# Five pairs of merge gate blocks as seven products of half matrices, computed ahead of the keys, values and queries

## The chip, the cores and the metric

The kernel runs on one core of a Trainium2 chip. The metric is the device time of one execution in microseconds (us). The core's engines run side by side, each through its own list of instructions in a fixed order: PE multiplies matrices (and loads the stationary operand, PEld), DVE (VectorE) and ACT (ScalarE) work elementwise, POOL (GpSimd) as well, and SP mainly issues DMA transfers. An instruction starts when the one before it on its engine is through and what it waits for on other engines and transfers has happened.

## The reference

One decoder layer for 1024 tokens of width 1024. A normalised input `h` is multiplied by `w_in`; the 3768 columns of the product feed two token mixers in parallel (NSA with compressed, selected and window attention; MLA with low-rank queries and keys) and the merge gates, which are the last 2048 columns. The gates weigh the two mixers, then come an output projection and a gated feed-forward part.

```
h = _rmsnorm(x, g_pre_mix[i])
proj = h @ w_in[i]
q_n, kv_n, gate_n, c_q, c_kv, k_r, merge = jnp.split(proj, offsets, axis=-1)
...
gm = jax.nn.sigmoid(merge...).reshape(B, T, 2, D)
merged = gm[:, :, 0] * (o_nsa @ w_br_nsa[i]) + gm[:, :, 1] * (o_mla @ w_br_mla[i])
x = x + _rmsnorm(merged @ w_o[i], g_post_mix[i])
h = _rmsnorm(x, g_pre_ffn[i])
u = _causal_dwconv(h @ w_up[i], w_conv[i], b_conv[i])
a, v = u[..., :D_FF], u[..., D_FF:]
x = x + _rmsnorm((jax.nn.gelu(a) * v) @ w_down[i], g_post_ffn[i])
```

## The kernel before

Precision: every float32 factor is held as two halves, a high one (`hh`, `whi`, `rh`, ...) and a low one (`hl`, `wlo`, `rl`, ...), and a product is three matmuls, high by high, high by low and low by high (`mm3`, L191). The halves come from `split_evac` (L197): ACT copies the value to the high half, then DVE subtracts the high half from the value. So each split is an ACT and a DVE instruction, in that order, and the second waits for the first. `h` lies transposed, features on partitions, as `hh[c]`, `hl[c]` for the two halves `c` of the tokens; the program prints them as `hh_122`, `hh_124` (high) and `hl_123`, `hl_125` (low).

Weights: `Weights` (L53) is a queue. A raw block of 128 columns (1024 rows, 512 KB) is loaded by SP into one of three buffers `wraw`, split into `whi`/`wlo` (two buffers each), and its raw buffer is given back (`done`). The queue runs in the order in which items are added.

A projection of one block, `fproj` (L436 to L449), is 2 token halves x 8 row blocks x 3 = 48 matmuls of 128x512. For a merge gate, `merge_evac` (L451) lets ACT take the sigmoid out of PSUM and issues the store to `gm_d`. There are sixteen such gate blocks.

The order of the work before: the input is normalised, gate 0 is computed, then MLA's queries, keys and values (`mla_q`, `mla_qt`, `mla_v`, `mla_k`, L488 to L543), which store their results to DRAM from SP (`q_d` L517, `v_d` L526, `k_d` L535, from the tiles `qx`, `vm`, `kx`, two buffers each). Gates 1 and 2 follow (L557), then the compressed keys (`kcT`), keys, values and queries, then gates 3 to 13 (L672), then attention, in which gates 14 and 15 are computed. When MLA's pool is closed behind it, its memory is given to later tiles; such a tile can be written once the store that reads the old one has landed.

Seven products: the up projection of the feed-forward part already multiplies pairs of blocks in this way (L1158 to L1450). A pair is the 1024 x 256 matrix of two column blocks, `a` and `v`; with the 1024 tokens it is a product of a 2 x 2 by a 2 x 2 matrix of halves. Instead of eight half products it uses seven, P1 to P7: the weights give sums S1 to S4 (`block_sum`), the tokens give sums T1 to T4 (`t_blocks`, L1239 to L1267, once), each sum is split into high and low, and the seven results are added up (U2, U3, C). One half product is 12 matmuls of 128x512, so a pair is 84 matmuls instead of 96. `prep` splits the next product's weight halves into `rh`, `rl` (4 buffers), 4 products ahead.

The order on each engine is set when the program is built: a scheduler that knows the operations' costs reorders the written order, within buffers and data dependences.

Of the kernel before, what the change touches and what calls it, by code (L numbers as in the profile page):

```python
# [17 lines left out]
T = 1024  # L18
# [111 lines left out]
        return self.items[i].hl  # L130


def attend(units, fills):
# [27 lines left out]
    for _, _, f in sorted(ev, key=lambda e: e[:2]):  # L161
        f()
# [3 lines left out]
def tile_hybrid_layer(ctx: ExitStack, tc: tile.TileContext, x, p, positions, g_pre_mix, w_in,  # L166
# [87 lines left out]
    for c0 in [0, 128, 256, 384] + [1720 + 128 * m for m in range(NM, 16)]:  # L254
# [193 lines left out]
    def fproj(evac):  # L448
        fproj2([evac])  # L449
# [219 lines left out]

    for f in range(4):  # L670
        fproj(q_evac(f))
    for m in range(NM, 14):  # L672
        fproj(merge_evac(m))


    def slope(h):
# [475 lines left out]
    def flat(ps):  # L1152
# [1 line left out]

    lo_k, hi_k = slice(0, 4), slice(4, 8)  # L1158
    block = dict(P1="A11", P2="A12", P3="S4", P4="A22", P5="S1", P6="S2", P7="S3")
    SEQ = [(f, p, block[p]) for f in range(1, NF)  # L1160
           for p in (("P1", "P6", "P7", "P5", "P2", "P4", "P3") if f > 1 else ("P1", "P2", "P3", "P5", "P6", "P7", "P4"))]
    WT, SS = {}, {}
    RING = 4

    def halves(src):
        hl = [ring([128, 4, 128], F32R, tag, bufs=RING) for tag in ("rh", "rl")]
        split_evac(*hl, src)
        return hl

    def pair(f):  # L1170
        return [it.raw.rearrange("p (k m) -> p k m", m=128) for it in up_pairs[f]]

    def block_sum(f, i):

        a, v = pair(f)
        out_ = SS[f, i] = ring([128, 4, 128], F32, f"S{i}")
        first, second, op = ((v[:, lo_k], v[:, hi_k], OP.add), (SS.get((f, 0)), a[:, lo_k], OP.subtract),
                             (a[:, lo_k], v[:, lo_k], OP.subtract), (a[:, hi_k], SS.get((f, 1)), OP.subtract))[i]
        nc.vector.tensor_tensor(out_, first, second, op=op)

    def prep(n):

        if n >= len(SEQ):
            return
        f, _, name = SEQ[n]
        a, v = pair(f)
        WT[n] = halves(SS[f, int(name[1]) - 1] if name[0] == "S" else
                       a[:, lo_k] if name == "A11" else a[:, hi_k] if name == "A12" else v[:, hi_k])
        if name in ("A12", "A22"):
            W.done()  # L1190
# [41 lines left out]
    takes = dict(P1="B11", P2="B21", P3="B22", P4="T4", P5="T1", P6="T2", P7="T3")  # L1232
# [6 lines left out]
    def t_blocks():  # L1239
# [29 lines left out]
    def product(ps, n, more=False):  # L1269
        wh, wl = WT.pop(n)  # L1270
        bh, bl = BB[takes[SEQ[n][1]]]
        for k in range(4):
            mm3(ps, wh[:, k], wl[:, k], bh[:, k], bl[:, k], not more and k == 0, k == 3, more)
# [101 lines left out]

    low, high = slice(2, 514), slice(514, 1026)
    for i in range(4):
        block_sum(1, i)
    X = [big(), big()]
    for c in (1, 0):  # L1380
        for s in range(2):
            for h, name in enumerate((("B11", "B21"), ("B12", "B22"))[c]):
                (wh, wl), (bh, bl) = W0[s][h], BB[name]
                for k in range(4):
                    mm3(X[s][:, c], wh[:, k], wl[:, k], bh[:, k], bl[:, k], h == k == 0, h == 1 and k == 3)
                if c == 0:
                    prep(2 * s + h)
    for s in range(2):
        nc.scalar.activation(CC[0][s][:, 2:], flat(X[s]), AF.Copy)
    t_blocks()  # L1390
    pieces = conv_pieces(0, CC[0])
    for f in range(1, NF):
        C = CC[f % 2]
        X = big()
        for s in range(7):
            n = 7 * (f - 1) + s
            pr = SEQ[n][1]
            if pr == "P1":
                product(X[:, 0], n)
            elif pr == "P2":  # L1400
                product(X[:, 0], n, more=True)
            elif pr == "P5":
                product(X[:, 1], n)
            elif pr == "P3" and f > 1:
                product(X[:, 1], n, more=True)
            elif pr == "P3":
                first = one()
                product(first, n)
            elif pr == "P6":
                six = one()  # L1410
                product(six, n)
            elif pr == "P7":
                seven = one()
                product(seven, n)
            else:
                product(seven, n, more=True)
            prep(n + RING)
            if s < 4 and f + 1 < NF:
                block_sum(f + 1, s)
            for run in pieces[s]:  # L1420
                run()
            if pr == "P1":
                e1 = ep([128, 512], F32, "e1")
                nc.scalar.activation(e1, X[:, 0], AF.Copy)  # L1424
            elif pr == "P2":
                nc.scalar.activation(C[0][:, low], X[:, 0], AF.Copy)
            elif pr == "P3" and f > 1:
                nc.vector.tensor_tensor(C[0][:, high], X[:, 1], U2, op=OP.add)
            elif pr == "P3":
                e3 = ep([128, 512], F32, "U3")  # L1430
                nc.scalar.activation(e3, first, AF.Copy)
            elif pr == "P6":
                U2 = ep([128, 512], F32, "U2")
                nc.vector.tensor_tensor(U2, six, e1, op=OP.add)
                if f == 1:
                    nc.vector.tensor_tensor(C[0][:, high], X[:, 1], U2, op=OP.add)
                    nc.vector.tensor_tensor(C[0][:, high], C[0][:, high], e3, op=OP.add)
            elif pr == "P7":
                U3 = ep([128, 512], F32, "U3")
                nc.vector.tensor_tensor(U3, seven, U2, op=OP.add)  # L1440
            if pr == ("P5" if f > 1 else "P7"):
                nc.vector.tensor_tensor(C[1][:, high], X[:, 1], U3, op=OP.add)
            elif pr == "P4":
                nc.vector.tensor_tensor(C[1][:, low], seven, U2, op=OP.add)
# [227 lines left out]
```

## Time and profile before

| what | us |
|---|---|
| median of three runs | 1791.93 (1789.28, 1799.06, 1791.93) |
| the profiled execution | 1793.26 |
| its span | 1791.5 |
| PE busy | 1724.0 (96%), 8585 matmuls |
| DVE busy | 1196.9 (67%) |
| ACT busy | 837.7 (47%) |
| POOL busy | 308.5 (17%) |

Busy times overlap. The span is the time from the first to the last instruction of the profiled execution; 1.8 us of the execution's time lies around it. The mean granted TensorE clock was 0.989 of full speed. In the profile a row names line, engine, operation and tiles (output, then inputs); "[2.10 <-DVE vm L199]" behind a row means that the engine had been idle for 2.10 us, and that the wait ended with the DVE instruction of line 199 that wrote `vm`.

### The profile page before, as it was taken

What the parts mean: (1) busy time and instruction counts of PE and PEld (TensorE: products, weight loads), DVE (VectorE), ACT (ScalarE), POOL (GpSimd) and SP (SyncE); (2) the same over time, 40 slices, a digit from 0 to 9 for tenths busy, and PEclk for the clock granted to TensorE, in tenths of its full rate; (3) what the DMA queues carried; (4) which work ended last, traced back from release to release, by engine and by line L of the source; (5) the groups of instructions that cost most, each with busy time, mean ns of one, the idle gap of its engine ahead of it and who ended that gap; (6) DMA issues with size and microseconds to landing.
All of it is one profiled execution on the core that took longest, in us unless ns stands there. A gap on an engine that the chain in (4) does not pass through costs nothing.

```text
span 1791.5 us, 23480 instructions
## 1 busy us (share of the span) xinstructions
PE 1724.0 (96%) x8585; PEld 1411.1 (79%) x8585; DVE 1196.9 (67%) x1875; ACT 837.7 (47%) x1498; POOL 308.5 (17%) x467
## 2 busy tenths in 40 slices
PE   8979999999999999999999989999999998999998
PEld 6868978887787787887778867888888876887886
DVE  6543431116888888787764787888888879768553
ACT  6442322115777766666542434444444443335321
POOL 3132000003555553333311000000000000001010
PEclk9999999999999999999999999999999999999999
DMA  5385122320001316657372112222223292438111
GB/s 193 89 245 143 48 58 84 94 77 24 2 1 36 106 58 181 151 146 190 110 252 99 36 59 87 79 82 94 72 83 95 71 340 94 137 117 291 55 59 47
DMA packets 182511, 191.94 MB, mean 107 GB/s; under 512 B 12804, under 2 KB 136124, under 8 KB 182396
## 3 DMA queue, kind: packets, MB, share of 16 engines
q1 hardware_dynamic: 175292, 180.91, 33.1%
q10 hardware_dynamic: 7104, 9.54, 1.7%
q8 instruction: 68, 1.11, 0.3%
q14 instruction: 47, 0.39, 0.1%
HBM read 142.96 MB, written 47.45 MB: 106 GB/s over the span
## 4 chain that ended last, share of the span: by engine, by line
PE 77%; DVE 8%; DMA 7%; ACT 3%; issue 2%; POOL 1%; SPq 1%; ACTq 0%; DVEq 0%; POOLq 0%
PE big L194 9%; PE big L193 9%; PE big L195 9%; PE pT L193 7%; PE pT L195 7%; PE pT L194 7%; PE pT L734 5%; PE one L193 3%; PE one L194 3%; PE one L195 3%; PE oT L744 3%; PE oT L743 3%; PE sc L797 1%; DVE wlo L199 1%; PE sc L790 1%
## 5 line engine op out<-in xcount | busy, mean ns | idle before, releaser
L235 POOL TENSOR_SCALAR stat<-stat 128x1 f32<-128x1 f32 (+1 forms) x48 | 19.4, 404 | 898.3 <-ACT yn L1130 632.2
L199 DVE TENSOR_TENSOR pl<-pT,ph 128x512 fp32r<-128x512 f32 (+1 forms) x244 | 149.4, 629 | 13.7 <-ACT ph L198 12.0
L198 ACT ACTIVATE ph<-pT 128x512 fp32r<-128x512 f32 (+1 forms) x244 | 130.1, 555 | 60.7 <-PE pT L734 52.9
L193 PE MATMUL pT<-hh,whi 128*128 128x512 f32 x384 | 151.4, 394 | 5.2 <-DVE vm L199 2.1
L195 PE MATMUL pT<-hh,wlo 128*128 128x512 f32 x384 | 151.0, 393 | 0.0
L194 PE MATMUL pT<-hl,whi 128*128 128x512 f32 x384 | 151.0, 393 | 0.0
L193 PE MATMUL big<-hh,rh 128*128 128x512 f32 x364 | 142.1, 391 | 2.0 <-ACT e L1424 0.8
L195 PE MATMUL big<-hh,rl 128*128 128x512 f32 x364 | 141.6, 390 | 1.0 <-DVE rl L199 1.0
L194 PE MATMUL big<-hl,rh 128*128 128x512 f32 x364 | 141.8, 390 | 0.0
L718 DVE TENSOR_REDUCE mx<-sc 128x1 f32<-128x640 f32 (+7 forms) x128 | 106.5, 834 | 34.6 <-PE sc L797 24.7
L107 DVE TENSOR_TENSOR wlo<-wraw,whi 128x1024 fp32r<-128x1024 f32 x26 | 31.9, 1226 | 140.8 <-ACT whi L106 140.7
L1286 DVE SCALAR_TENSOR_TENSOR u<-C,wcT,u 128x1024 f32<-128x1024 f32 x88 | 110.8, 1278 | 3.4 <-ACT u L1282 3.4
L194 PE MATMUL big<-wlo,whi 128*128 128x512 f32 x242 | 97.5, 403 | 9.4 <-DVE wlo L199 9.3
L198 ACT ACTIVATE rh<-S 128x512 fp32r<-128x512 f32 x84 | 52.6, 629 | 99.9 <-PE big L194 85.3
L195 PE MATMUL big<-whi,wlo 128*128 128x512 f32 x242 | 96.1, 397 | 0.0
L193 PE MATMUL big<-whi 128*128 128x512 f32 x242 | 92.2, 397 | 1.2 <-ACT whi L198 1.2
L193 PEld LDWEIGHTS pT<-hh,whi 128*128 128x128 f32 x384 | 72.9, 190 | 21.5 <-DVE vm L199 2.5
L198 ACT ACTIVATE rh<-wraw 128x512 fp32r<-128x512 f32 x67 | 41.9, 630 | 92.7 <-PE big L194 41.8
L195 PEld LDWEIGHTS pT<-hh,wlo 128*128 128x128 f32 x384 | 72.9, 190 | 15.3
L194 PEld LDWEIGHTS pT<-hl,whi 128*128 128x128 f32 x384 | 72.8, 190 | 15.1
L193 PEld LDWEIGHTS big<-hh,rh 128*128 128x128 f32 x364 | 68.2, 188 | 17.7 <-ACT e L1424 1.2
L195 PEld LDWEIGHTS big<-hh,rl 128*128 128x128 f32 x364 | 68.3, 188 | 15.6 <-DVE rl L199 1.4
(484 smaller groups left out, 4769.1 us busy)
## 6 DMA issues: line engine op xcount, KB each, us to landing
wraw<-in_w_up_dram SPq DMA_DIRECT2D x44, 512.0 KB, 3.8
wraw<-in_w_in_dram SPq DMA_DIRECT2D x24, 512.0 KB, 4.3
g<-gm_d SPq DMA_DIRECT2D x48, 256.0 KB, 3.2
wraw<-in_w_down_dram SPq DMA_DIRECT2D x47, 256.0 KB, 3.2
g_d<-u SPq DMA_DIRECT2D x22, 512.0 KB, 2.8
wraw<-g_d SPq DMA_DIRECT2D x36, 256.0 KB, 3.3
xt<-in_x_dram SPq DMA_DIRECT2D x16, 512.0 KB, 6.9
gm_d<-gms ACTq DMA_DIRECT2D x16, 512.0 KB, 3.0
```

The costliest lines, as they stand in the source:

```text
L107: nc.vector.tensor_sub(lo, raw, f32(hi))
L193: nc.tensor.matmul(ps, lh, rh, start=start, stop=False, skip_group_check=more)
L194: nc.tensor.matmul(ps, lh, rl, start=False, stop=False, skip_group_check=more)
L195: nc.tensor.matmul(ps, ll, rh, start=False, stop=stop, skip_group_check=more)
L198: nc.scalar.activation(hi, ps, AF.Copy)
L199: nc.vector.tensor_sub(lo, ps, f32(hi))
L235: nc.gpsimd.tensor_scalar(st, st, EPS, None, op0=OP.add)
L718: nc.vector.tensor_reduce(u.nm[:, r:r + 1], src, axis=AX.XY, op=OP.max, negate=True)
L734: nc.tensor.transpose(pT[:m, r], cols(r), ident)
L743: nc.tensor.matmul(oT[:, a:], v, ph, start=first, stop=False)
L744: nc.tensor.matmul(oT[:, a:], v, pl, start=False, stop=last)
L1286: nc.vector.scalar_tensor_tensor(u[s], C[s][:, 2 - sh:2 - sh + T], wcT[:, 2 - sh, ch:ch + 1], u[s], op0=OP.mult, op1=OP.add)
```

## The change

The seven products become a class `Seven`, which the feed-forward part now uses as well, with the orders `FIRST` for its first pair and `LATER` for the others as before. A second user of the class is new: gates 3 to 12, as five pairs. For them the token sums T1 to T4 are made by `t_block` on DVE (three additions or subtractions of 128x1024 for each half, then a split), through one buffer `sum`. Gates 1, 2 and 13 stay plain blocks, and all of this comes directly behind MLA; gates 14 and 15 stay in attention. The tiles lie in three pools, `tA` (T1 to T4), `ringA` (S0 to S3, `rh`, `rl`, a fourth raw buffer) and `eA` (`sum` and the parts of the result). The sigmoid of a quarter is taken out of PSUM, of the other three after the additions.

```diff
+class Seven:
+    TAKES = dict(P1=("A11", "B11"), P2=("A12", "B21"), P3=("S4", "B22"), P4=("A22", "T4"),
+                 P5=("S1", "T1"), P6=("S2", "T2"), P7=("S3", "T3"))
+    FIRST = ("P1", "P2", "P3", "P5", "P6", "P7", "P4")
+    LATER = ("P1", "P6", "P7", "P5", "P2", "P4", "P3")
+    RING = 4
...
+    def halves(self, src):
+        hl = [self.ring([128, 4, 128], F32R, tag, bufs=self.RING) for tag in ("rh", "rl")]
+        self.split(*hl, src)
+        return hl
...
+    def product(self, ps, n, more=False):
+        wh, wl = self.WT.pop(n)
+        bh, bl = self.BB[self.TAKES[self.seq[n][1]][1]]
+        for k in range(4):
+            self.mm3(ps, wh[:, k], wl[:, k], bh[:, k], bl[:, k], not more and k == 0, k == 3, more)
+
+    def pair(self, f, X, bank, ep, C, c11, hook):
...
-    NM = 3
-    for c0 in [1720 + 128 * m for m in range(1, NM)] + [512, 640, 768, 1024]:
+    EARLY, PAIRED = (1, 2, 13), range(3, 13)
+    for m in EARLY:
+        W.add(Item(in_cols(1720 + 128 * m), 1024))
+    gate_pairs = [[W.add(Item(in_cols(1720 + 128 * m), 1024, custom=True)) for m in (m_, m_ + 1)] for m_ in PAIRED[::2]]
+    for c0 in [512, 640, 768, 1024]:
         W.add(Item(in_cols(c0), 1024))
...
+    def t_block(out_, plus, minus):
+        for ks in (slice(0, 2), slice(2, 4)):
+            (ah, al), (bh, bl) = ([f32(b[:, ks]) for b in BA[n]] for n in (plus, minus))
+            sum_ = eA([128, 2, 512], F32, "sum")
+            nc.vector.tensor_tensor(sum_, ah, bh, op=OP.subtract)
+            nc.vector.tensor_tensor(sum_, sum_, al, op=OP.add)
+            nc.vector.tensor_tensor(sum_, sum_, bl, op=OP.subtract)
+            split_evac(BA[out_][0][:, ks], BA[out_][1][:, ks], sum_)
+
+    fproj(merge_evac(EARLY[0]))
+    t_block("T1", "B12", "B11")
+    fproj(merge_evac(EARLY[1]))
+    t_block("T2", "B22", "T1")
+    t_block("T3", "B22", "B12")
+    fproj(merge_evac(EARLY[2]))
+    for i in range(4):
+        gates7.block_sum(0, i)
+    for n in range(Seven.RING):
+        gates7.prep(n)
+    t_block("T4", "B21", "T2")
+    for f in range(len(gate_pairs)):
+        tl = [gmp([128, T], F32, "gms", bufs=2) for _ in range(2)]
+        gates7.pair(f, two_banks(), bank, eA, [(c[:, :512], c[:, 512:]) for c in tl],
+                    lambda out_, ps: nc.scalar.activation(out_, ps, AF.Sigmoid), lambda s: None)
+        nc.scalar.activation(tl[1], tl[1], AF.Sigmoid)
+        nc.scalar.dma_start(gm_d[PAIRED[2 * f + 1]], tl[1])
+        nc.scalar.activation(tl[0][:, 512:], tl[0][:, 512:], AF.Sigmoid)
+        nc.scalar.dma_start(gm_d[PAIRED[2 * f]], tl[0])
...
-    for m in range(1, NM):
-        fproj(merge_evac(m))
...
-    for m in range(NM, 14):
-        fproj(merge_evac(m))
```

On DVE, behind MLA's last split (`qx`), the kernel before splits a weight block and then clears the tiles of the compressed keys and the queries:

```order
L199 TENSOR_TENSOR kx<-pT,kx 128x512
L199 TENSOR_TENSOR qx<-sc,qx 96x8x128
L107 TENSOR_TENSOR wlo<-wraw,whi 128x1024
L631 MEMSET KAc_1314 128x64
L632 MEMSET KBc_1316 128x64
```

At the same place the changed kernel has the sums of the weights (`S`, L170), of the tokens (`sum`, L675 to L677) and the splits (L309):

```order
L309 TENSOR_TENSOR qx<-sc,qx 96x8x128
L107 TENSOR_TENSOR wlo<-wraw,whi 128x1024
L170 TENSOR_TENSOR S_1532<-wraw 128x512
L170 TENSOR_TENSOR S_1536<-wraw 128x512
L170 TENSOR_TENSOR S_1534<-S_1532,wraw 128x512
L309 TENSOR_TENSOR T1l<-sum,T1h 128x1024
L309 TENSOR_TENSOR rl<-wraw,rh 128x512
L170 TENSOR_TENSOR S_1538<-wraw,S_1534 128x512
L309 TENSOR_TENSOR rl<-wraw,rh 128x512
L675 TENSOR_TENSOR sum<-hh_122,hh_124 128x1024
```

From the second `S` to the last `T4l` there are 59 such instructions in a row on DVE, 30 of 128x512 and 29 of 128x1024, and none of other work but the first additions of the results.

On PE, behind the plain blocks, the kernel before goes on with `hh`, `hl` by `whi`, `wlo` (compressed keys):

```order
L195 MATMUL pT<-hh_124,wlo 128x512
L193 MATMUL pT<-hh_122,whi 128x512
L194 MATMUL pT<-hl_123,whi 128x512
L195 MATMUL pT<-hh_122,wlo 128x512
L193 MATMUL pT<-hh_122,whi 128x512
```

In the changed kernel the products of the first pair stand there; P1 and P3 take halves of `h`, and the 25th matmul takes T2:

```order
L303 MATMUL pT<-hh_122,rh 128x512
L304 MATMUL pT<-hl_123,rh 128x512
L305 MATMUL pT<-hh_122,rl 128x512
L303 MATMUL pT<-T2h,rh 128x512
L303 MATMUL sc<-hh_124,rh 128x512
L304 MATMUL sc<-hl_125,rh 128x512
```

The last product of the first pair, P4, takes T4; in front of it stand the products P1, P6, P7 and P5 of the second pair:

```order
L304 MATMUL sc<-hl_125,rh 128x512
L305 MATMUL sc<-hh_124,rl 128x512
L303 MATMUL pT<-T4h,rh 128x512
L304 MATMUL pT<-T4l,rh 128x512
L305 MATMUL pT<-T4h,rl 128x512
L303 MATMUL pT<-T4h,rh 128x512
```

From the first matmul of the first product to the first that reads the second half of T4, 126 matmuls are issued.

## Rows read from the trace of the kernel before

**Rows 1.** The page: busy time of each engine, and the chain's shares.
```profile
PE 1724.0 (96%) x8585; PEld 1411.1 (79%) x8585; DVE 1196.9 (67%) x1875; ACT 837.7 (47%) x1498; POOL 308.5 (17%) x467
...
PE 77%; DVE 8%; DMA 7%; ACT 3%; issue 2%; POOL 1%; SPq 1%; ACTq 0%; DVEq 0%; POOLq 0%
```

**Rows 2.** Stretches: us, busy per engine, PEclk, DMA share, GB/s.
```profile
core 0: us, PE busy (x) PEld busy (x) DVE busy (x) ACT busy (x) POOL busy (x), PEclk, DMA share, GB/s
...
124.85:140.00 15.15, 13.05 (x49) 10.31 (x50) 3.83 (x4) 3.86 (x6) 2.63 (x4) 0.89 0.82 220
...
229.20:404.00 174.80, 174.79 (x764) 144.42 (x765) 29.72 (x33) 39.19 (x55) 2.40 (x4) 0.99 0.27 79
...
1022.90:1062.00 39.10, 31.58 (x119) 23.32 (x117) 38.99 (x47) 18.50 (x25) 0.00 (x0) 0.92 0.17 54
1062.00:1420.00 358.00, 356.69 (x1571) 294.57 (x1571) 298.89 (x388) 162.10 (x224) 0.00 (x0) 1.00 0.26 84
```

**Rows 3.** Timeline of DVE in gates 3 to 13: start, us.
```profile
308.16 1.23 DVE L107 TENSOR_TENSOR wlo<-wraw,whi 128x1024 fp32r<-128x1024 f32 x1 [9.65 <-ACT whi L106]
...
395.20 1.23 DVE L107 TENSOR_TENSOR wlo<-wraw,whi 128x1024 fp32r<-128x1024 f32 x1 [9.65 <-ACT whi L106]
```

**Rows 4.** Timeline of ACT, one row for each pair of the feed-forward part.
```profile
1130.38 0.58 ACT L1424 ACTIVATE e<-big 128x512 f32<-128x512 f32 x1
...
1149.42 0.58 ACT L1424 ACTIVATE e<-big 128x512 f32<-128x512 f32 x1
```

**Rows 5.** Timeline of ACT, the ends of plain blocks behind MLA.
```profile
139.87 1.06 ACT L106 ACTIVATE whi<-wraw 128x1024 fp32r<-128x1024 f32 x1 [3.15 <-PE pT L194]
...
161.63 1.06 ACT L106 ACTIVATE whi<-wraw 128x1024 fp32r<-128x1024 f32 x1 [2.22 <-PE pT L194]
```

**Rows 6.** Timeline of SP: start and us of the issue of MLA's last store.
```profile
142.59 1.02 SPq L517 DMA_DIRECT2D q_d<-qx  x1
```

**Rows 7.** Line 517, the stores of qx: issue to landing.
```profile
L517 SPq DMA_DIRECT2D q_d<-qx x8: 323/1050/1767, 89.9 to 142.6; - x8
...
DMA to landing us min/median/max: 7.1/8.9/10.7
```

**Rows 8.** Timeline of DVE behind MLA.
```profile
140.96 1.23 DVE L107 TENSOR_TENSOR wlo<-wraw,whi 128x1024 fp32r<-128x1024 f32 x1 [2.99 <-ACT whi L106]
...
145.38 0.48 DVE L687 MEMSET QB<- 64x512 f32 x1 [2.19 <-DMA v_d<-vm]
```

**Rows 9.** Timeline of DVE at the start of the feed-forward pairs.
```profile
1033.41 0.69 DVE L199 TENSOR_TENSOR rl<-wraw,rh 128x512 fp32r<-128x512 f32 x1
1034.02 1.22 DVE L199 TENSOR_TENSOR T3l<-wlo,T3h 128x1024 fp32r<-128x1024 f32 x1
1035.15 1.28 DVE L1286 SCALAR_TENSOR_TENSOR u<-C,wcT,u 128x1024 f32<-128x1024 f32 x1
```

**Rows 10.** Groups of ACT in the feed-forward pairs: busy, mean ns.
```profile
L198 ACT ACTIVATE T4h<-wlo 128x1024 fp32r<-128x1024 f32 x1 | 1.1, 1058 | 1.3 <-DVE wlo L1249 1.3
```

**Rows 11.** Timeline of PE, its waits at the start of the feed-forward pairs.
```profile
1037.69 0.50 PE L195 MATMUL big<-hh,rl 128*128 128x512 f32 x1 [0.97 <-DVE rl L199]
...
1042.27 0.50 PE L193 MATMUL big<-hh,rh 128*128 128x512 f32 x1 [0.79 <-ACT e L1424]
...
1045.24 0.79 PE L195 MATMUL one<-T2h,rl 128*128 128x512 f32 x1 [2.23 <-DVE rl L199]
...
1052.34 0.47 PE L193 MATMUL one<-T4h,rh 128*128 128x512 f32 x1 [0.74 <-DVE U L1440]
...
1057.65 0.50 PE L193 MATMUL one<-T3h,rh 128*128 128x512 f32 x1 [2.33 <-DVE C L1444]
```

**Rows 12.** Stretches behind waits of PE; columns as in rows 2.
```profile
133.80:137.20 3.40, 3.40 (x10) 2.66 (x9) 0.45 (x1) 1.02 (x1) 0.00 (x0) 0.50 0.79 238
...
1045.20:1048.60 3.40, 3.36 (x8) 2.69 (x9) 3.40 (x5) 1.50 (x2) 0.00 (x0) 0.50 0.00 0
```

More of the change, by code (lines that the diff above doesn't have):

```diff
@@ L130, in get, with __init__, raw, block_sum @@
         return self.items[i].hl
+class Seven:
[4 more added lines that the diff above has]
+    RING = 4
+    def __init__(self, nc, W, pairs, ring, BB, mm3, split):
+        self.nc, self.W, self.ring, self.BB, self.mm3, self.split = nc, W, ring, BB, mm3, split
+        self.pairs, self.lo, self.hi = pairs, slice(0, 4), slice(4, 8)
+        self.seq = [(f, p) for f in range(len(pairs)) for p in (self.LATER if f else self.FIRST)]
+        self.WT, self.SS = {}, {}
+        for i, it in enumerate(it for its in pairs for it in its):
+            it.ahead = int(i > 2)
+            it.home = (ring, "wraw", 1) if i % 4 == 3 else None
+    def raw(self, f):
+        return [it.raw.rearrange("p (k m) -> p k m", m=128) for it in self.pairs[f]]
+    def halves(self, src):
+        hl = [self.ring([128, 4, 128], F32R, tag, bufs=self.RING) for tag in ("rh", "rl")]
+        self.split(*hl, src)
+        return hl
+    def block_sum(self, f, i):
+        if f >= len(self.pairs):
+            return
+        (a, v), lo, hi, SS = self.raw(f), self.lo, self.hi, self.SS
+        out_ = SS[f, i] = self.ring([128, 4, 128], F32, f"S{i}")
+        first, second, op = ((v[:, lo], v[:, hi], OP.add), (SS.get((f, 0)), a[:, lo], OP.subtract),
+                             (a[:, lo], v[:, lo], OP.subtract), (a[:, hi], SS.get((f, 1)), OP.subtract))[i]
+        self.nc.vector.tensor_tensor(out_, first, second, op=op)
+    def prep(self, n):
+        if n >= len(self.seq):
+            return
+        f, p = self.seq[n]
+        name, (a, v) = self.TAKES[p][0], self.raw(f)
+        self.WT[n] = self.halves(self.SS[f, int(name[1]) - 1] if name[0] == "S" else
+                                 a[:, self.lo] if name == "A11" else a[:, self.hi] if name == "A12" else v[:, self.hi])
+        if name in ("A12", "A22"):
+            self.W.done()
+    def product(self, ps, n, more=False):
[4 more added lines that the diff above has]
+    def pair(self, f, X, bank, ep, C, c11, hook):
+        nc, (((C11, C12), (C21, C22))) = self.nc, C
+        def add(out_, a, b):
+            nc.vector.tensor_tensor(out_, a, b, op=OP.add)
+        for s in range(7):
+            n = 7 * f + s
+            p = self.seq[n][1]
+            if p in ("P1", "P5"):
+                self.product(X[:, p == "P5"], n)
+            elif p == "P2" or p == "P3" and f:
+                self.product(X[:, p == "P3"], n, more=True)
+            elif p == "P3":
+                three = bank()
+                self.product(three, n)
+            elif p == "P6":
+                six = bank()
+                self.product(six, n)
+            elif p == "P7":
+                seven = bank()
+                self.product(seven, n)
+            else:
+                self.product(seven, n, more=True)
+            self.prep(n + self.RING)
+            if s < 4:
+                self.block_sum(f + 1, s)
+            hook(s)
+            if p == "P1":
+                e1 = ep([128, 512], F32, "e1")
+                nc.scalar.activation(e1, X[:, 0], AF.Copy)
+            elif p == "P2":
+                c11(C11, X[:, 0])
+            elif p == "P3" and f:
+                add(C12, X[:, 1], U2)
+            elif p == "P3":
+                e3 = ep([128, 512], F32, "U3")
+                nc.scalar.activation(e3, three, AF.Copy)
+            elif p == "P6":
+                U2 = ep([128, 512], F32, "U2")
+                add(U2, six, e1)
+                if not f:
+                    add(C12, X[:, 1], U2)
+                    add(C12, C12, e3)
+            elif p == "P7":
+                U3 = ep([128, 512], F32, "U3")
+                add(U3, seven, U2)
+            elif p == "P4":
+                add(C21, seven, U2)
+            if p == ("P5" if f else "P7"):
+                add(C22, X[:, 1], U3)
@@ L253, in tile_hybrid_layer @@
                        [[N_IN, 128], [128 * N_IN, 4], [256, 2], [1, 128]]), 1024))
-    for c0 in [0, 128, 256, 384] + [1720 + 128 * m for m in range(NM, 16)]:
+    for c0 in [0, 128, 256, 384] + [1720 + 128 * m for m in (14, 15)]:
         W.add(Item(in_cols(c0), 1024))
@@ L545, in tile_hybrid_layer @@
     a0.close()
+    tA = Pool("tA", side="left")
+    ringA = Pool("ringA", side="left")
+    eA = Pool("eA", side="left")
+    BA = {n: [tA([128, 4, 512], F32R, n + tag) for tag in "hl"] for n in ("T1", "T2", "T3", "T4")}
+    for c in range(2):
+        for h in range(2):
+            ks = slice(4 * h, 4 * h + 4)
+            BA[f"B{h + 1}{c + 1}"] = hh[c][:, ks], hl[c][:, ks]
+    gates7 = Seven(nc, W, gate_pairs, ringA, BA, mm3, split_evac)
+    def t_block(out_, plus, minus):
[25 more added lines that the diff above has]
+        nc.scalar.dma_start(gm_d[PAIRED[2 * f]], tl[0])
+    for pl in (eA, ringA, tA):
+        pl.close()
     vp0 = Pool("vp0", side="left")
@@ L1158, in tile_hybrid_layer @@
     lo_k, hi_k = slice(0, 4), slice(4, 8)
[L1159 to L1190, printed above, removed]
+    BB = {}
+    up7 = Seven(nc, W, up_pairs[1:], ring, BB, mm3, split_evac)
     W0 = {}
     def prep0(s):
-        raw = pair(0)[s]
-        W0[s] = halves(raw[:, lo_k]), halves(raw[:, hi_k])
+        raw = up_pairs[0][s].raw.rearrange("p (k m) -> p k m", m=128)
+        W0[s] = up7.halves(raw[:, lo_k]), up7.halves(raw[:, hi_k])
         W.done()
@@ L1267, in t_blocks @@
             put("T4", ks, total(nc.vector, ("whi", "wlo")[j], b21h, (OP.subtract, t2[j]), (OP.add, b21l)))
[L1269 to L1273, printed above, removed]
     def conv_pieces(f, C):
@@ L1377, in tile_hybrid_layer @@
     for i in range(4):
-        block_sum(1, i)
+        up7.block_sum(0, i)
     X = [big(), big()]
@@ L1393, in tile_hybrid_layer, with hook @@
         C = CC[f % 2]
[L1394 to L1419, printed above, removed]
+        def hook(s):
             for run in pieces[s]:
                 run()
[L1422 to L1444, printed above, removed]
             if f == NF - 1 and s == 2:
@@ L1449, in tile_hybrid_layer @@
                 ready(s - 4)
+        up7.pair(f - 1, big(), one, ep, [(c[:, low], c[:, high]) for c in C],
+                 lambda out_, ps: nc.scalar.activation(out_, ps, AF.Copy), hook)
         pieces = conv_pieces(f, C)
```

8 lines of the change are left out of this document (2 added, 6 removed).

## The prediction

> **What bounds the kernel now.** I read the page first. The reader is to see in it that PE is busy for 1724.0 of 1791.5 us and makes 77% of the chain, while DVE, busy for 1196.9 us, makes 8% of it [rows 1]. So a matmul taken away is worth its time wherever PE runs without a gap, and DVE costs nothing as long as PE has other work. Then I took the stretches one by one. In the one that holds gates 3 to 13, PE is busy for 174.79 of 174.80 us and DVE for 29.72: only PE counts there, and DVE has room. In the stretch right behind MLA's start of gate 1, from 124.85 to 140.00, the transfers are dense (share 0.82, 220 GB/s), and at the start of the feed-forward pairs DVE is full (38.99 of 39.10 us) and PE is not (31.58) [rows 2]. The last one is the nearest thing to the new stage that the trace has: the same seven products, with their T blocks made just in time. Last I read the pace of PE, and on SP, DVE and PE who waits for whom around the place to which the gates go.
>
> **What it removes.** In the gate stretch one block's split follows the other at equal distance: nine such rows from 308.16 to 395.20 are eight blocks, 87.04 / 8 = 10.88 us for 48 matmuls, 0.2267 us each [rows 3]. In the steady feed-forward pairs it is 1149.42 - 1130.38 = 19.04 us for 84 matmuls, 0.2267 us as well [rows 4], with PE busy for 356.69 of 358.00 us there [rows 2]. So the seven products run at the same pace once they are fed, and five pairs save 5 x 12 = 60 matmuls: 60 x 0.2267 = 13.6 us. This is the most that the change can give.
>
> **What it adds, and where.** Behind MLA, DVE gets one row of 59 instructions: the splits and sums of the first pair's weights, part of the second's, and T1 to T4. The change shows 30 of 128x512 and 29 of 128x1024. On a full DVE one starts 0.61 us behind a 128x512 (1033.41 to 1034.02) and 1.13 us behind a 128x1024 (1034.02 to 1035.15) [rows 9]; so the row takes 30 x 0.61 + 29 x 1.13 = 51.1 us. Beside it stand waits for ACT: where a T's low half follows directly on the last sum, DVE waits for ACT's copy of 1.06 us [rows 10]. That is so three times (second half of T1, first of T2, second of T4), and half so once or twice more: together about 4 us. 55 us in all.
>
> The starts of DVE in rows 9 lie closer than its durations (1.22 and 0.69 us). The Trainium skill, page VectorE: DVE Perf Modes, section The DRAIN you can't avoid, says that the next operation does not start until the pipe is empty. The trace does not agree: each of these starts comes 0.08 to 0.09 us ahead of the end of the one before. By that rule the row would be priced by durations, 30 x 0.69 + 29 x 1.22 = 56.1 us, and the end result would be 5 us later; I go by the starts.
>
> When can the row begin? Its second instruction, a weight sum, writes into memory that MLA's tiles had, and the last store to read them there is the last `q_d` of `qx`. It is issued at 142.59 [rows 6], and such a store lands 7.1 to 10.7 us after its issue, 8.9 in the median [rows 7]: 149.7 to 153.3. I take 153.3, since the transfers are dense at this time and the others of MLA are in flight beside it. That such reuse does stop DVE is seen at the same place now: a MEMSET of `QB` waits 2.19 us for `v_d<-vm` [rows 8]. What stands ahead of it, one weight split, is over at 142.2 [rows 8]. So the row is done at 153.3 + 55 = 208.4.
>
> When does PE want the results? Gate 1 ends at 139.87, and two plain blocks later, at 161.63, the third does [rows 5]; this is also the time at which the first of the seven products can start in the changed kernel, as three plain blocks stand in front. The first use of T4's second half comes 126 matmuls later: 161.6 + 126 x 0.2267 = 190.2. The weight halves for P1 and P3 (the third to the tenth instruction of the row) are ready at about 160, so PE can start, and then waits at T2, T3 and T4 in turn, since from there on it eats the blocks faster than DVE makes them. However the idle time is spread, PE stands at T4's second half at 208.4 and not at 190.2: **18.2 us** lost. On PE the whole queue is behind that wait: the other pairs, then keys, values and queries, so nothing fills it.
>
> Behind T4, DVE has some weight halves to catch up. At the same point of the feed-forward part, PE waits 0.74 us at T4 and then 2.33 us in the pair behind it [rows 11]: 3.1 us. Its bounds are 0 (the later pairs there lose nothing [rows 2]) and 7.5 us, all that PE lost in that start (39.10 - 31.58 [rows 2]).
>
> The clock: behind the 2.10 us wait at 132.69, which is one of PE's waits on MLA, and behind the 2.23 us wait at 1045.24 [rows 11], PE runs for 3.4 us at a granted clock of 0.50, that is 1.2 GHz, in place of 2.4 [rows 12]; half of it is lost, 1.7 us. Drops behind the first waits cost nothing, for PE waits again at the next T block anyway; only the one behind T4 counts: 1.7 us (bounds 0 and 1.7 for each of four waits, 6.8).
>
> **What comes at no cost.** ACT gets the copies of the sums and weights, the parts `e` and `U3` and sigmoids of SBUF; it is busy for 39.19 of 174.80 us in the gate stretch [rows 2], and only the copies in front of a DVE split are on the path (counted). SP issues as many gate weights as before, only sooner, so the next blocks come behind MLA's stores in its queue; with a share of 0.27 in the gate stretch [rows 2] there is room once MLA's stores are out. The keys, values, queries and their small loads on ACT's queue move back as a whole and keep their order; the gate stretch hid nothing that they need, since PE was full in it and DVE nearly idle. The first sums of T1 go between MLA's splits on DVE, two of them ahead of a `qx`: DVE is busy for 3.83 of 15.15 us there [rows 2], so they cost nothing, or 2 x 1.13 = 2.3 us if they meet a split for which PE waits. What the gates cover today is nothing.
>
> **Sum.** -13.6 + 18.2 + 3.1 + 1.7 = +9.4 us against the profiled execution of 1793.3 us: 1802.7. That execution lies 1.3 us above the median of the runs, 1791.9, which gives 1801.3; I say 1802.
>
> **Rivals.**
> Rival A, the cover holds (faster). If DVE could begin the row at 142 (behind the weight split) and PE's first 24 matmuls and the four products of the second pair that are drawn ahead of P4 cover most of the T blocks, PE waits about as much as at the start of the feed-forward pairs, 7.5 us, or less. For it: the scheduler placed products in front of P4 for just that; three plain blocks, 32.6 us, stand in front. Against it: the row is 55 us long, and 32.6 us of cover run mostly before it can begin. With 4 us of waits: -13.6 + 4 = -9.6, 1784.
>
> Rival B, the waits cancel the saving (no change). The store lands early (149.7), or the weight sum doesn't wait for it but only for the one before, so that DVE works through part of the row by 153: begun at 142.2, it ends at 197.2, and PE loses 7.0 at T4, with 3.1 + 1.7 behind it: -13.6 + 11.8 = -1.8; halfway between that and the forecast, +4. So 1790 to 1797, say 1794.
>
> Rival C, the clock is paid in full (slower still). Every wait of over 2 us at T2, T3 and T4 brings a stretch at half clock that is not hidden by the next wait, and one more in the pairs behind: 4 x 1.7 = 6.8 in place of 1.7, and 1807; with the bound of 7.5 for the pairs behind, 1811. For it: rows 12 stand right behind waits of 2.10 and 2.23 us. Against it: most of the time behind the first waits is waiting for DVE anyhow. The Trainium skill, page TensorE: Matmul & The Clock Gate, section HAM oscillation, describes a kernel whose matmuls come in bursts between waits and which pays for the low clock at every burst. Rows 12 agree for single waits; no run here shows a chain of them.
>
> Rival D, it doesn't do what it says: the products are not fed and PE keeps 96 matmuls a pair's time. The steady pairs of the feed-forward part [rows 4] leave this no more than a few parts in a hundred.
>
> **How the numbers follow.** The forecast (DVE's row decides, start 149.7 to 153.3 and small terms within their bounds: 1797 to 1808) gets 0.54, rival C 0.13, rival B 0.19, rival A 0.13, rival D 0.01. About 9 us, 0.5%, is what a measurement of this kernel can tell from no change (the three runs spread over 9.8 us), so the border to slower is 1801, next to the forecast; two thirds of its weight lie above: slower 0.36 + 0.13 + 0.01 = 0.50, rounded up to 0.52 for the price of rows by durations; same 0.18 + 0.19 = 0.35 less some of it, 0.34; faster 0.14. The range is 1788 to 1811: it holds the forecast, rival B and most of C, and leaves A out. The forecast's own range is 1797 to 1808.
>
> **What would show it.** In the profile after: a row of T and S instructions on DVE without gaps from about 153 to 208, its start behind a wait for `q_d<-qx`; PE's waits in front of rows with `T2h`, `T3h`, `T4l`, released by DVE, 18 us together; pairs 19.04 us apart behind them; the keys starting some 100 us later than now; no change in length behind the gates. The forecast is wrong if DVE starts on the row before 150, if PE's waits at T blocks are under 10 us together, or if PE waits at each head of the later pairs.

## The result and the profile after

The changed kernel takes 1800.52 us in the median of 20 runs, the kernel before 1789.44 us: a ratio of 1.0062, 95% interval 1.0047 to 1.0076, or 11.1 us more. The forecast was 1802 us, from +9.4. One of the 12 executions of the run with four pairs behind five plain blocks ran at a granted clock of 0.847 and took 1901.49 us; it is left out of that run's median below.

The profiled execution has a span of 1801.3 us. On the page, DVE has grown to 1274.0 us and to 10% of the chain [rows 1]:

```profile
PE 1720.6 (96%) x8525; PEld 1403.2 (78%) x8525; DVE 1274.0 (71%) x1978; ACT 860.7 (48%) x1532; POOL 310.7 (17%) x467
...
PE 75%; DVE 10%; DMA 8%; ACT 3%; issue 2%; POOL 1%; SPq 1%; DVEq 0%; POOLq 0%; ACTq 0%
```

PE has 60 matmuls fewer but is busy for only 3.4 us less, since more of them ran at half clock. Where the rest went stands in the stretches from the start of gate 1 to the fourth pair (columns as in [rows 2]):

```profile
119.46:149.00 29.54, 27.79 (x121) 22.37 (x121) 10.76 (x12) 7.98 (x11) 0.00 (x0) 1.00 0.85 235
149.00:154.58 5.58, 5.58 (x25) 4.61 (x25) 5.58 (x8) 1.64 (x3) 0.00 (x0) 1.00 0.35 91
154.58:203.62 49.04, 35.83 (x129) 26.16 (x127) 45.01 (x50) 17.01 (x24) 0.00 (x0) 0.84 0.21 65
203.62:212.20 8.58, 8.29 (x18) 5.71 (x19) 3.27 (x5) 2.14 (x3) 0.00 (x0) 0.51 0.17 63
212.20:229.00 16.80, 16.31 (x72) 13.14 (x70) 9.25 (x15) 6.63 (x11) 0.00 (x0) 1.00 0.38 118
229.00:250.00 21.00, 19.35 (x85) 15.70 (x85) 11.06 (x17) 8.04 (x12) 0.00 (x0) 1.00 0.23 70
```

The third row runs from the first matmul of the first product to the first that reads T4's second low half. The latter is one matmul further than the 126 of the section on the change, so 49.04 us stand there in place of 127 x 0.2267 = 28.8. In the fourth, PE is busy but at half clock. The last is about one pair: PE is busy for 19.35 us and has one wait.

DVE's timeline shows why. The columns are start, duration, engine, line, operation and tiles:

```profile
131.94 1.23 DVE L107 TENSOR_TENSOR wlo<-wraw,whi 128x1024 fp32r<-128x1024 f32 x1 [0.77 <-ACT whi L106]
137.51 0.69 DVE L170 TENSOR_TENSOR S<-wraw 128x512 f32<-128x512 f32 x1 [4.34 <-DMA q_d<-qx]
147.32 0.69 DVE L170 TENSOR_TENSOR S<-wraw 128x512 f32<-128x512 f32 x1 [9.12 <-DMA q_d<-qx]
147.93 0.69 DVE L170 TENSOR_TENSOR S<-S,wraw 128x512 f32<-128x512 f32 x1
...
202.34 1.22 DVE L309 TENSOR_TENSOR T4l<-sum,T4h 128x1024 fp32r<-128x1024 f32 x1 [1.12 <-ACT T4h L308]
```

The row of sums and splits waits 9.12 us for the last store of `qx`, starts at 147.32 and ends at 203.56 (202.34 + 1.22). SP issued that store at 135.99:

```profile
135.99 0.87 SPq L630 DMA_DIRECT2D q_d<-qx  x1
```

PE's waits in the same time and behind it:

```profile
149.00 0.50 PE L303 MATMUL pT<-hh,whi 128*128 128x512 f32 x1 [1.65 <-ACT gms L570]
164.56 0.80 PE L303 MATMUL pT<-T2h,rh 128*128 128x512 f32 x1 [4.38 <-ACT rh L308]
179.90 0.50 PE L303 MATMUL pT<-T3h,rh 128*128 128x512 f32 x1 [2.00 <-ACT T3h L308]
195.76 0.80 PE L303 MATMUL pT<-T4h,rh 128*128 128x512 f32 x1 [3.06 <-ACT T4h L308]
197.02 0.80 PE L304 MATMUL pT<-T4l,rh 128*128 128x512 f32 x1 [0.46 <-DVE T4l L309]
202.36 0.79 PE L303 MATMUL pT<-T4h,rh 128*128 128x512 f32 x1 [2.84 <-ACT T4h L308]
203.62 0.80 PE L304 MATMUL pT<-T4l,rh 128*128 128x512 f32 x1 [0.47 <-DVE T4l L309]
206.41 0.80 PE L303 MATMUL sc<-hh,rh 128*128 128x512 f32 x1 [0.29 <-ACT rh L308]
229.01 0.50 PE L303 MATMUL sc<-hh,rh 128*128 128x512 f32 x1 [0.49 <-ACT rh L308]
249.99 0.50 PE L303 MATMUL sc<-hh,rh 128*128 128x512 f32 x1 [1.64 <-DVE S L170]
```

All of them stand in front of a T block or a head of a pair, except the first. Most end with a copy on ACT, not with DVE; but these copies in turn wait for DVE's sums, as the last one of T4 does:

```profile
201.25 1.06 ACT L308 ACTIVATE T4h<-sum 128x1024 fp32r<-128x1024 f32 x1 [5.55 <-DVE sum L677]
```

The first wait comes from ACT itself: the sigmoid that frees a PSUM bank was queued behind a copy of a weight half that waited for the same store:

```profile
147.31 1.15 ACT L308 ACTIVATE rh<-wraw 128x512 fp32r<-128x512 f32 x2 [13.44 <-DMA q_d<-qx]
148.37 0.58 ACT L570 ACTIVATE gms<-pT 128x512 f32<-128x512 f32 x1
```

**The account of the stretch.** From the first matmul of gate 1 to the first matmul of attention (`sc<-KA,QA`), the kernel before needs 405.67 - 124.85 = 280.8 us, the changed one 412.53 - 119.46 = 293.1: +12.3. Its parts: -13.6 for 60 matmuls; +20.2 to T4 (49.04 - 28.8); +1.65 behind ACT; +4.2 at half clock behind T4 (half of the stretch to 212.20); +2.4 for waits at later heads (0.29 + 0.49 + 1.64). That makes +14.9. The wait of 2.10 us and the drop of 1.7 us [rows 12] that the kernel before has in gate 1 are absent: -3.8. So +11.1, and 1.2 us are left over. This is the wait in the kernel before:

```profile
132.69 0.51 PE L193 MATMUL pT<-hh,whi 128*128 128x512 f32 x1 [2.10 <-DVE vm L199]
```

In none of the traces of the variants below does PE wait for more than 0.8 us inside gate 1, and that of the move alone needs 406.57 - 128.09 = 278.5 us for the same stretch. Against it the changed kernel takes 14.6 us more, and the parts without gate 1 make 14.9. With one trace of the kernel before, it stays open whether its wait is usual.

The two profiled spans differ by 9.8 us, not 12.3. MLA ended 5.4 us sooner in this execution. In the executions of the variants below it ended as late as 128.93 (second try of the addresses) or 127.28 (first try) with the same work, so I don't count that as an effect of the change. About 3 us are lost behind the first matmul of attention (1388.8 against 1385.8 us to the end), where this execution has a stretch at half clock that the other has not (935 to 950, clock 0.77):

```profile
935.00:950.00 15.00, 9.49 (x37) 7.41 (x35) 10.02 (x9) 5.65 (x10) 4.31 (x8) 0.77 0.46 166
```

### The profile page after: what moved, and what is told of

The parts are those of the page before. It is cut to its first block, busy times and chain, and to the rows that moved or that the text cites. A ratio compares the mean times of both kernels' runs of the same rounds, so it can differ in the third digit from the quotient of the medians.

```text
span 1801.3 us, 23532 instructions
## 1 busy us (share of the span) xinstructions
PE 1720.6 (96%) x8525; PEld 1403.2 (78%) x8525; DVE 1274.0 (71%) x1978; ACT 860.7 (48%) x1532; POOL 310.7 (17%) x467
## 4 chain that ended last, share of the span: by engine, by line
PE 75%; DVE 10%; DMA 8%; ACT 3%; issue 2%; POOL 1%; SPq 1%; DVEq 0%; POOLq 0%; ACTq 0%
PE big L304 9%; PE big L303 9%; PE big L305 9%; PE pT L303 5%; PE pT L304 5%; PE pT L305 5%; PE pT L885 5%; PE one L303 3%; PE one L304 3%; PE one L305 3%; PE oT L895 3%; PE oT L894 3%; PE sc L948 1%; DVE wlo L309 1%; DMA g<-gm_d 1%
## 5 line engine op out<-in xcount | busy, mean ns | idle before, releaser
L309 DVE TENSOR_TENSOR pl<-pT,ph 128x512 fp32r<-128x512 f32 (+1 forms) x244 | 149.7, 630 | 13.8 <-ACT ph L308 12.0
L308 ACT ACTIVATE rh<-S 128x512 fp32r<-128x512 f32 x104 | 65.1, 628 | 120.6 <-PE big L304 80.4
L308 ACT ACTIVATE rh<-wraw 128x512 fp32r<-128x512 f32 x82 | 51.3, 631 | 131.7 <-PE big L304 43.0
L303 PE MATMUL pT<-hh,whi 128*128 128x512 f32 x224 | 88.6, 395 | 4.1 <-ACT gms L570 1.6
L305 PE MATMUL pT<-hh,wlo 128*128 128x512 f32 x224 | 87.9, 392 | 0.0
L304 PE MATMUL pT<-hl,whi 128*128 128x512 f32 x224 | 87.8, 392 | 0.0
L309 DVE TENSOR_TENSOR rl<-S,rh 128x512 fp32r<-128x512 f32 x104 | 71.0, 686 | 21.2 <-ACT rh L308 21.2
L304 PEld LDWEIGHTS big<-hl,rh 128*128 128x128 f32 x364 | 68.5, 188 | 14.5 <-DVE hl L309 0.4
L309 DVE TENSOR_TENSOR rl<-wraw,rh 128x512 fp32r<-128x512 f32 x82 | 56.2, 687 | 21.1 <-ACT rh L308 21.1
L308 ACT ACTIVATE whi<-wraw 128x1024 fp32r<-128x1024 f32 x40 | 42.1, 1058 | 56.9 <-DVE wraw L1464 27.2
```

The source lines that it names most:

```text
L303: nc.tensor.matmul(ps, lh, rh, start=start, stop=False, skip_group_check=more)
L304: nc.tensor.matmul(ps, lh, rl, start=False, stop=False, skip_group_check=more)
L305: nc.tensor.matmul(ps, ll, rh, start=False, stop=stop, skip_group_check=more)
L308: nc.scalar.activation(hi, ps, AF.Copy)
L309: nc.vector.tensor_sub(lo, ps, f32(hi))
```

## The experiments

Theory: the first pair's T blocks come too late, because DVE's row starts at the landing of MLA's last store and is 55 us long. Rivals: the place itself costs; each pair loses by its own waits; the clock. All times are medians, ratios against the kernel before in the same job.

### The move alone

```diff
-    EARLY, PAIRED = (1, 2, 13), range(3, 13)
+    EARLY = range(1, 14)
...
+    for m in EARLY:
+        fproj(merge_evac(m))
```

> Gates 1 to 13 as plain blocks ahead of the keys, no seven products: the move alone. Theory (PE runs out of T blocks, the place itself costs nothing): PE stays full behind MLA, the time is that of the kernel before, 1789 us, within 5 us. Rival (the place costs): the +11.1 us of the change and the 13.6 us saved would both lie in the move, and this run takes about 1789 + 25 = 1814 us.

Measured: 1791.47 us, ratio 1.0018 (1.0004 to 1.0033), 2 to 3 us more. From 130 to 345 us PE is full:

```profile
130.00:345.00 215.00, 214.72 (x1059) 181.44 (x1058) 53.60 (x80) 51.09 (x77) 13.56 (x29) 1.00 0.36 101
```

That is inside the 5 us of the theory. The loss to be explained is 11.1 + 13.6 = 24.7 us; the upper end of the interval, 5.9 us, is about a quarter of it, so the products bring the rest. Where the 2 to 3 us lie is open: in the trace, the stretch from gate 1 to attention is 2.3 us shorter than in the kernel before.

### Four pairs, behind three plain blocks and behind five

```diff
-    EARLY, PAIRED = (1, 2, 13), range(3, 13)
+    EARLY, PAIRED, LATE = (1, 2, 13), range(3, 11), (11, 12)
...
```

> Four pairs instead of five; gates 11 and 12 are plain blocks behind the pairs, so three plain blocks stand in front as in the changed kernel. Theory (the loss is made once, at T2 to T4 of the first pair): 48 matmuls saved instead of 60, so 2.7 us more than the changed kernel: 1803 us. Rival (each pair loses by its own waits): the loss of 24.7 us shrinks to four fifths, 19.8, less the 10.9 saved: +8.9, 1798 us.

Measured: 1803.22 us, ratio 1.0082 (1.0053 to 1.0112). This is the value of the theory, 1.0076; the rival's 1798 us, 1.0048, lies just outside the interval of these six executions. The trace says it more plainly: from the first product to the second low half of T4, PE needs 204.26 - 154.72 = 49.54 us, as in the changed kernel (49.04). The loss is made once.

```diff
-    EARLY, PAIRED = (1, 2, 13), range(3, 13)
+    EARLY, PAIRED = (1, 2, 11, 12, 13), range(3, 11)
...
```

> The same four pairs, with gates 11 and 12 as plain blocks in front of them: five plain blocks of cover. Theory: PE comes to T4 21.8 us later, at about 205 us, when DVE's row is through (203 in the changed kernel), so nearly all of the 20 us wait goes: 1789 - 10.9 + 3 to 8 us of small waits and clock, 1781 to 1787 us, about 18 us below the run with three blocks in front. Rival (it is the number of products or the place): no difference to that run, 1798 to 1803 us.

Measured: 1788.10 us, ratio 0.999 (0.9972 to 1.0008): 15.1 us below the run with three blocks, where 18 were expected, and 1 us above the expected range. T3 and T4 don't stop PE any more. DVE stood still for 14.59 us before it could go on with its row, as the copy of a weight half waited; by the profile the load of its block (`wraw`), not a store of MLA, ended that wait:

```profile
152.99 1.15 ACT L308 ACTIVATE rh<-wraw 128x512 fp32r<-128x512 f32 x2 [13.19 <-DMA wraw<-in_w_in_dram]
153.66 0.69 DVE L309 TENSOR_TENSOR rl<-wraw,rh 128x512 fp32r<-128x512 f32 x1 [14.59 <-ACT rh L308]
```

```profile
158.41 0.80 PE L305 MATMUL pT<-hh,wlo 128*128 128x512 f32 x1 [2.05 <-DVE wlo L107]
189.60 0.50 PE L303 MATMUL pT<-T2h,rh 128*128 128x512 f32 x1 [2.81 <-ACT rh L308]
```

The second wait stands in front of T2, but T2 was there: its last split began at 175.81. PE waited for a weight half whose copy (188.92) stands on ACT behind that of T3's second half (186.98), which had waited for DVE. The expectation of the run after the second try below takes this wait for one at T2, and the 14.59 us for one on the stores.

### Three pairs behind seven plain blocks

```diff
-    EARLY, PAIRED = (1, 2, 13), range(3, 13)
+    EARLY, PAIRED = (1, 2, 9, 10, 11, 12, 13), range(3, 9)
...
```

(with the addresses of the second try below)

> Three pairs behind seven plain blocks, same addresses: 36 matmuls saved, 8.2 us. Theory: PE comes to the first product 43.5 us later than with three blocks, all T blocks are ready, no wait at T2 to T4 is left and about 2 to 3 us of small waits at the heads remain: 1789.4 - 8.2 + 3 = 1784 us. Rival (the loss is not made by the T blocks): 1789 us or more.

Measured: 1780.31 us, ratio 0.9946 (0.9929 to 0.9964), 8.7 us faster than the kernel before, and below the expectation; the 36 matmuls are worth 8.2. No wait at a T block is left. From gate 1 to attention the trace needs 393.00 - 123.08 = 269.9 us, 8.6 less than that of the move alone. With enough plain blocks in front, the saving comes in full.

### The start of DVE's row: three tries

The tiles of the pairs lie from the bottom up, MLA's tiles (`kx`, `vm`, `qx`) in the middle of the same memory. First try, the pools turned:

```diff
-    tA = Pool("tA", side="left")
     ringA = Pool("ringA", side="left")
     eA = Pool("eA", side="left")
+    tA = Pool("tA", side="left")
...
```

> Five pairs as in the changed kernel; only the order of the three pools is turned, so that the weight sums and splits get memory that MLA's tiles did not have, and T1 to T4 come last. Theory (DVE's row starts late because its second instruction waits for the last q_d store): the weight part starts at about 137 instead of 147, T1's split now waits for stores instead, and T4 is ready 5 to 9 us earlier: 1792 to 1796 us. Rival (the start is not what sets T4): 1800 us.

Measured: 1798.55 us, ratio 1.0051 (1.0029 to 1.0072), a miss. The weight sums started sooner, at 141.64 in an execution whose MLA ended 7.8 us later; but T4 was ready only 1 us sooner (83.0 us behind the start of gate 1, 84.1 in the changed kernel). T1's copy (150.43) did not wait for stores, as had been expected: it stands on ACT behind a sigmoid that waited 4.84 us for PE. And the weight block of the second pair came late:

```profile
149.37 0.60 ACT L570 ACTIVATE gms<-pT 128x512 f32<-128x512 f32 x1 [4.84 <-PE pT L305]
150.43 1.06 ACT L308 ACTIVATE T1h<-sum 128x1024 fp32r<-128x1024 f32 x1 [0.46 <-ACT gms L570]
151.53 1.23 DVE L309 TENSOR_TENSOR T1l<-sum,T1h 128x1024 fp32r<-128x1024 f32 x1 [3.92 <-ACT T1h L308]
160.82 0.69 DVE L170 TENSOR_TENSOR S<-wraw 128x512 f32<-128x512 f32 x1 [5.73 <-DMA wraw<-in_w_in_dram]
```

Second try, `ringA` lowest and T1 as the highest T block:

```diff
+    ringA = Pool("ringA", side="left")
     tA = Pool("tA", side="left")
-    ringA = Pool("ringA", side="left")
...
-    BA = {n: [...] for n in ("T1", "T2", "T3", "T4")}
+    BA = {n: [...] for n in ("T4", "T3", "T2", "T1")}
```

> Five pairs behind three plain blocks, with DVE's order the same as in the changed kernel; only the addresses differ (weight tiles lowest, T1 highest), so that neither the first pair's weight sums and splits nor T1's first half wait for the last q_d store. Theory A (the wait for that store alone sets T4): T4 comes 9 us sooner, 1791 us. Theory B (behind it stands a second wall, the landing of the second pair's weight block, whose sum stands between T1's two halves on DVE; in the run with turned pools it held DVE until 33.5 us after the start of gate 1, in the changed kernel the row came there at 35.5): T4 comes about 2 us sooner, 1798 us.

Measured: 1802.37 us, ratio 1.0059 (1.0038 to 1.008). The edit did not do what it was made for: T1 now lay where `qx` had been, and its copy waited for the very store. So it decides nothing between the two theories:

```profile
156.25 1.06 ACT L308 ACTIVATE T1h<-sum 128x1024 fp32r<-128x1024 f32 x1 [14.00 <-DMA q_d<-qx]
```

The same addresses with four pairs behind five plain blocks:

> Four pairs behind five plain blocks, with the same addresses. In the run with five blocks DVE stood 14.6 us on a weight split that waited for MLA's stores, and PE then waited 2.05 us for a weight split, 2.81 us at T2 and 3.3 us at later heads. Theory: the 2.05 and part of the 2.81 go: 1784 to 1787 us, faster than the kernel before by about 4 us. Rival (the waits come from the blocks' loads, not the stores): 1788 us as before.

Measured: 1788.87 us, ratio 0.9991 (0.9976 to 1.0006), as without them, and the rival's value. PE waits 3.95 us in front of T2 here, again for a weight half; T1's first split came at 149.25, 14.92 us after DVE had run dry. T1's copy waited for the last store, and the block of the weight half behind it landed at the same time, so freeing the weight tiles alone could help little:

```profile
148.17 1.06 ACT L308 ACTIVATE T1h<-sum 128x1024 fp32r<-128x1024 f32 x1 [14.60 <-DMA q_d<-qx]
149.91 1.15 ACT L308 ACTIVATE rh<-wraw 128x512 fp32r<-128x512 f32 x2 [0.20 <-DMA wraw<-in_w_in_dram]
```

Third try, T1 and `ringA` lowest, T2 to T4 in MLA's memory, `sum` above it:

```diff
     tA = Pool("tA", side="left")
     ringA = Pool("ringA", side="left")
+    tB = Pool("tB", side="left")
     eA = Pool("eA", side="left")
-    BA = {n: [tA(...) ...
+    BA = {n: [(tA if n == "T1" else tB)(...) ...
```

> Five pairs behind three plain blocks, a second try at the start of DVE's row: T1 and the weight tiles lie lowest, T2 to T4 where MLA's tiles were, the sum buffer above. In the run before, the wait for q_d had only moved to T1's copy on ACT; here T1, the first weight sums and splits wait for no store, T2 waits for earlier ones. Theory A (start of the row sets T4): T1's second half and T2's first are done when the second pair's block lands, T4 comes about 10 us sooner, 1788 to 1791 us. Theory B (the second pair's block lands no sooner and DVE has as much to do behind it): 1797 to 1800 us.

Measured: 1785.72 us, ratio 0.9967 (0.9952 to 0.9983), faster than theory A said. By an edit that only moves tiles the change turns from 11 us slower to 5 to 6 us faster (a difference of 0.95 points of the ratio). DVE's order is another one as well: the scheduler put the sums and splits of T1 in front of the weight sums. So T1 is made while MLA ends, the weight sum comes without a wait, and DVE's row ends at 190.2 with only one wait for a transfer, 0.39 us. That is 65.4 us behind the start of gate 1, in place of 84.1:

```profile
130.67 1.23 DVE L309 TENSOR_TENSOR T1l<-sum,T1h 128x1024 fp32r<-128x1024 f32 x1 [0.26 <-ACT T1h L308]
...
142.26 1.29 DVE L170 TENSOR_TENSOR S<-wraw 128x512 f32<-128x512 f32 x2
...
153.29 0.69 DVE L170 TENSOR_TENSOR S<-wraw 128x512 f32<-128x512 f32 x1 [0.39 <-DMA wraw<-in_w_in_dram]
...
189.02 1.22 DVE L309 TENSOR_TENSOR T4l<-sum,T4h 128x1024 fp32r<-128x1024 f32 x1 [0.52 <-ACT T4h L308]
```

Of the T blocks, PE then waits only for the second half of T4; 2.3 us at the heads of later pairs stay:

```profile
189.04 0.49 PE L303 MATMUL pT<-T4h,rh 128*128 128x512 f32 x1 [2.75 <-ACT T4h L308]
190.30 0.50 PE L304 MATMUL pT<-T4l,rh 128*128 128x512 f32 x1 [0.76 <-DVE T4l L309]
```

Theory A stands; theory B, that the second pair's block holds the row anyway, falls in this form. What the new addresses give by themselves and what DVE's new order gives was not tried apart.

### Without T4

```diff
-    t_block("T4", "B21", "T2")
+    BA["T4"] = BA["T2"]
```

> The changed kernel without the sum T4: the last product of each pair takes T2 in its place, so 8 of DVE's 59 instructions and 2 copies are left out. Theory (PE's idle time at T4 and the half clock behind it are the price of DVE's row): the 7.1 us of waits at T4 and most of the 6 us lost at 1.2 GHz around them go, 1788 to 1792 us. Rival (PE's loss lies before T4 or in the later pairs): 1797 us or more.

Measured: 1788.86 us, ratio 0.9989 (0.9973 to 1.0006), inside the expectation. (This kernel leaves out the sum T4, so its gates are not those of the layer.) Eight instructions of DVE, 9 us of its row, and what they bring behind them at half clock make up the whole difference between the changed kernel and the kernel before. Up to the wait at T3 nothing changes (4.37 us at T2, 1.92 at T3).

### Four pairs, five plain blocks, and the third addresses

> The same addresses with four pairs behind five plain blocks. Theory: DVE's row is through before PE needs T2 to T4; of the waits of the earlier runs with five blocks (2.05 us for a weight split, 2.8 to 4.0 at T2, 3.3 at later heads, half clock behind two of them) the first two go: 1783 to 1785 us. Rival (only more plain blocks help): 1788 us.

The edit is that of the run with five plain blocks together with that of the third try.

Measured: 1781.31 us, ratio 0.9942 (0.992 to 0.9965), about 10 us faster than the kernel before and below the expectation; the saving is 48 x 0.2267 = 10.9. From gate 1 to attention the trace needs 394.33 - 126.56 = 267.8 us, 10.7 less than that of the move alone. PE is full all through the gates:

```profile
135.00:300.00 165.00, 164.50 (x739) 135.47 (x738) 105.52 (x150) 57.70 (x84) 25.91 (x33) 1.00 0.41 119
```

DVE's row ends at 191.6, and T4 is first read at 206.14. DVE still waits 4.00 us for a weight half whose block has to land, but T1 and the first half of T2 are made by then, and PE never stops for it. This version and the one with three pairs beat both kernels; their intervals overlap.

## Why the prediction was right

- **The saving.** 60 matmuls at 0.2267 us. The runs without waits at T blocks show it: 8.2 us expected for 36 and 8.7 measured, 10.9 for 48 and about 10 measured. Right.
- **The start of DVE's row.** Forecast from the start of gate 1: 153.3 - 124.85 = 28.4 us; measured 147.32 - 119.46 = 27.9. (By the clock of this execution the row begins before 150, which was named as a sign of being wrong; but gate 1 began 5.4 us sooner too.) The named cause, the last `q_d` store, stands in the row as its releaser, 11.3 us behind its issue, a little above the largest value that I had.
- **The length of the row.** Forecast 55 us, measured 56.2. The starts lie 0.61 us behind a 128x512 on this full DVE too, so the price by starts holds, not that by durations; the waits for ACT are three of 1.12 us and one of 0.30. Where an operation works on the tile `sum` that the one directly before it used, it starts only at that one's end: 159.16, 160.42 and 161.68 are 1.26 us apart, not 1.13. The section of the Trainium skill that the prediction quotes (page VectorE: DVE Perf Modes, The DRAIN you can't avoid) goes on to say that a next operation that is not held starts earlier. With that the starts here agree, 0.08 us ahead of the end, so the prediction read only half of it.
- **The loss up to T4.** Forecast 18.2, measured 20.2. PE's waits at T blocks are 13.2 us of it, where 18 were named; the other 7 are matmuls at half clock between the waits, which cost nothing more, as DVE sets the end. PE started sooner against the row than reckoned: 154.58 - 147.32 = 7.3 us behind its start, forecast 161.6 - 153.3 = 8.3. The row was 1.2 us longer. The run without T4 and the third addresses both show that this is the price.
- **Behind T4.** 2.4 us of waits in place of 3.1. The clock is the term that was mis-sized: 4.2 us in place of 1.7. PE ran at a granted clock of about 0.5, 1.2 GHz, from T4's first half on and stayed there for 8.58 us after the last wait at T4, longer than the 3.4 us of [rows 12]. This was a part of rival C. PE did wait at each head of the later pairs that the timeline shows, which was named as a sign of being wrong; but these waits come to 2.4 us, and the loss had been made before them.
- **The wait on ACT.** 1.65 us at a PSUM bank were not foreseen. I had asked what is queued behind the waiting instruction on DVE, not on ACT, where `rh` waits for the same store.
- **What comes at no cost.** The move costs 2 to 3 us by itself, where I had none. Its cause is open.
- **Gate 1's wait and its drop of the clock,** 3.8 us, were counted as staying; they are absent. That the total came within 2 us of the forecast is partly luck: T4, ACT and the clock behind T4 together cost 6.2 us more than reckoned, the heads 0.7 less, and these 3.8 us set off most of it.
- Of the rivals, A and B were ruled out for these addresses only: with the third addresses the kernel lands between them. D fell: a later pair keeps PE busy for 19.35 us (19.04 forecast), where 96 matmuls would take 21.8. One slip in the chances: 0.18 + 0.19 is 0.37, not 0.35.

## What to carry to other kernels

Fewer matmuls pay only where their operands can be made while PE has other work. Count the preparing engine's instructions from the moment at which the first of them may run to the moment at which PE reads the last, and put that much other work in between. That moment may be set by an address: a tile in memory that an earlier stage is still storing from waits for the store (9.12 us here), and here another placement of the pools, with the order on DVE that came with it, was worth 15 us.

## What had not been expected of the hardware

TensorE stayed at half clock through a stretch in which it was busy for 8.29 of 8.58 us (203.62 to 212.20), behind four waits of 0.46 to 3.06 us that ended between 195.76 and 203.62; behind single waits the stretch at half clock had been 3.4 us [rows 12]. The length of a wait did not tell by itself whether the clock fell. It fell behind the wait of 2.00 us at T3 (second and third line) but not behind that of 1.64 us at the head of the fifth pair (first line):

```profile
250.00:256.80 6.80, 6.80 (x29) 5.41 (x30) 4.21 (x6) 3.38 (x5) 0.00 (x0) 1.00 0.56 175
179.00:182.40 3.40, 2.50 (x9) 2.02 (x10) 3.40 (x6) 1.48 (x2) 0.00 (x0) 0.85 0.10 40
182.40:185.80 3.40, 3.40 (x12) 2.66 (x11) 3.33 (x3) 0.63 (x1) 0.00 (x0) 0.65 0.29 114
```

Nor did it fall behind the wait of 2.81 us (at 189.60) in the first run with four pairs behind five plain blocks:

```profile
189.60:193.00 3.40, 3.40 (x15) 2.71 (x16) 3.40 (x5) 1.44 (x3) 0.00 (x0) 1.00 0.33 130
193.00:196.40 3.40, 3.40 (x17) 2.82 (x16) 3.40 (x5) 2.34 (x4) 0.00 (x0) 1.00 0.00 0
```
